# Half products for four of the `down` tiles and a third pair of `wno`, with two moved steps, in a one-core decoder layer

## The chip, the cores and the metric

The kernel runs on one core of one Trainium2 chip. The metric is the device time of one execution in microseconds (us). Three runs of the kernel before took 679.52, 680.35 and 680.2 us, so the median is 680.2 us.

The core has five engines with a queue each: TensorE (PE in the profile, its weight loads PEld), VectorE (DVE), ScalarE (ACT), GpSimd (POOL) and SyncE (SP). An engine works through its own queue in order, and waits at an instruction until the semaphores that this instruction names are there. Transfers are issued by SP and by POOL. TensorE writes its results into PSUM, eight banks per partition that hold 512 float32 values each; DVE and ACT read and write PSUM as well as SBUF.

## The reference

One decoder layer for 512 tokens of 1024 features: a norm, one wide projection, a pooling mixer and a sparse attention, gates that merge the two, an output projection, and a gated MLP with a short convolution. What the change touches:

```
x = x + (gate_pool * y_pool + gate_nsa * y_nsa) @ w_out      # y_nsa = heads @ w_nsa_out
h = rms_norm(x, ffn_norm_g)
gate_pre, val = split(h @ w_up)                              # 2 x 2816 columns
y = silu(causal_dwconv(gate_pre, conv_w, conv_b)) * val
x = x + y @ w_down                                           # 2816 = 22 tiles of 128 rows
```

All values are float32. The kernel keeps tokens in the free dimension, so a matrix is `out[128 features, 512 tokens] += w[128 x 128] x[128, 512]` over tiles of 128 features.

## The kernel before, in words

**Precision.** Every factor is split into a rounded high part and a low remainder (`split`: ACT makes the high part, DVE subtracts). A full-width step is then three matmuls of 512 columns: high by high, high by low, low by high (`mm3`). In some places the low part is made by a transfer that adds (`split_by_dma`: two ACT operations and a POOL transfer, nothing on DVE).

**Half products.** Some products are done two by two in Winograd's form of Strassen's scheme: a pair of output tiles, the contraction cut in two and the tokens cut in two, so that seven products of half the width (256 columns) stand where eight would. It needs sums of weight tiles and sums of input halves, which DVE makes. `product` runs one such half product: over `n` tiles, three matmuls of 256 columns each. A product whose `k0` is false does not begin a new sum, but adds to what lies in the bank; so ACT first copies an earlier product from its bank to the one that continues it. The MLP's `up` tiles 1 to 21 (`up_fast`), the last 8 of the 22 `down` tiles (`dz_fast`) and the first two of four pairs of `wno`, the attention's output projection (`FASTM = (0, 1)`), run so.

**The order of the `wno` and `out` stage.** The four pairs of `wno` come one after the other; a fast pair leaves its last two half products in `held`, to run inside the next pair. Each gives two merged tiles `mh[f]`, `ml[f]`, eight in all. `out` contracts over these eight. Its output tiles 0 and 4 begin with their weights and six of the eight steps each, then the last two steps follow (`begin`). After it come the norm's sum of squares, `norm_rstd` and `up` tile 0, which runs as two full products (`up_plain`): gate half, value half. Within the value half, after seven of its eight steps, TensorE broadcasts the norm's factor (`bcast_rstd`: `diag` tiles made by ACT and DVE, two matmuls, one ACT copy to `rb`).

**The order of the MLP.** `up` tiles 1 to 21 follow. `down` over its first 14 tiles is cut into `GROUPS`, of 5, 5 and 4 tiles; each group gives eight steps (`dn_group`), one per output tile: load the weights, split them, 15 (or 12) matmuls of 512 columns into the two-bank PSUM tile with the tag `sc`, and a DVE addition to `x2[f]`. A group is put on the list `fills` at the `up` tile given in `AT`, and `FILL` says how many steps of the list go before an `up` tile and at three places inside it, where TensorE has to wait for a copy otherwise. What is left of the list runs after `up` tile 21, and then `dz_fast` does the last 8 tiles. `y_sums` makes the sums of `y` halves that `dz_fast` needs.

**The planner.** No engine's order is written out fully. Every operation is noted with a price and with what it depends on (`Plan.note`), and `Plan.run` orders each engine's queue by due times; TensorE's order within the main stream is that of the program. PSUM tiles count as a whole in these dependences, unless their name is in `fine`; then it goes by columns. SBUF tiles come from 60 `page` buffers and three rings of three for weights (`wraw`, `whi`, `wlo`). `AHEAD` is the number of pages that must be left free when weights for half products are fetched ahead. All instructions are emitted at one place, so they all bear line 431 in the profile, and have to be told apart by their tiles.

Of the kernel before, what the change touches and what calls it, by code (L numbers as in the profile page):

```python
# [9 lines left out]
F32R = mybir.dt.float32r  # L10
I32 = mybir.dt.int32
AF = mybir.ActivationFunctionType
# [3 lines left out]
P = 128  # L16
T = 512
NT = 4
D = 1024
KD = 8  # L20
# [3 lines left out]
FF = 2816  # L24
KF = 22
LAST = 14
GROUPS = ((0, 5), (5, 10), (10, 14))
EPS = 1e-6
BIG = 1e30

# [23 lines left out]
RINGS = {"wraw": 3, "whi": 3, "wlo": 3}  # L54
PLAIN = (0,)
DIRECT = (0,)
FASTM = (0, 1)
AT = (6, 12, 16)
FILL = {f: (0, 0, 0, 0) for f in range(22)}
FILL.update({f: (0, 1, 1, 0) for f in (7, 10, 13, 16,)})  # L60
FILL.update({f: (0, 1, 0, 0) for f in (6, 8, 9, 11, 12, 14, 15, 17, 18, 19,)})
TRIES = 12
RESERVE = 3
CUTS = (1, 2)
# [4 lines left out]
SHARE = 1.5  # L69
LANDS = (0.8, 0.8, 1.2, 1.2, 2.0, 2.0)  # L70
TRIALS = ((0.5, RATE), (0.8, RATE), (1.4, RATE), (0.8, 0.9 * RATE))
AHEAD = 4
RUN = 12


# [357 lines left out]

@with_exitstack
def hybrid_layer(ctx: ExitStack, tc: tile.TileContext, xT, xa, pos, par, cst, poolw, w1, wa, wb, wf,
                 wpo, wno, wout, wup, wdn, wdz, out):
    nc = tc.nc
    pl = Plan(nc)
    PE, ACT, DVE, POOL, SP = pl.engines
# [8 lines left out]
    def page(name, shape=(P, T), dt=F32):  # L448
        return pl.tile(sb, shape, dt, name, "pg", PAGES)
# [59 lines left out]
    H2 = T // 2  # L509
# [18 lines left out]
    w2 = R("w2").rearrange("p (a b) -> p a b", a=2)  # L528
# [4 lines left out]
    pt = bank("mm")  # L533
# [61 lines left out]
    rb = keep("rb", (P, T))  # L595
# [42 lines left out]
    A, KQ, KH, KL = (ang[:, i] for i in range(4))  # L638
# [55 lines left out]
    for t in range(NT):  # L694
        pt = bank("mm")
# [593 lines left out]
    for f in (0, 4):  # L1289
        wh, wl = weights(flat(wout[f]), 1024, "v")  # L1290
        begin[f] = wh, wl, any_bank()
        mm3(begin[f][2], wh, wl, mh, ml, 0, 6, nk=KD)
    for f in (0, 4, 1, 5, 2, 6, 3, 7):
        xres = page("xres")
        with pl.behind(tail):
# [37 lines left out]
        ACT.activation(t, t, AF.Silu)  # L1333
        return t

    yth, ytl, ylast = {}, {}, {}

    def y_sums(k):
        b1, b2 = ylast[k], ylast[k + 4]
        ta, tb = page("ta"), page("tb")  # L1340
        DVE.tensor_sub(ta[:, :H2], b1[:, :H2], b1[:, H2:])
        DVE.tensor_sub(tb[:, :H2], b2[:, H2:], b1[:, H2:])
        DVE.scalar_tensor_tensor(ta[:, H2:], ta[:, :H2], -1.0, b2[:, H2:], op0=ALU.mult, op1=ALU.subtract)
        DVE.scalar_tensor_tensor(tb[:, H2:], ta[:, H2:], -1.0, b2[:, :H2], op0=ALU.mult, op1=ALU.subtract)
# [12 lines left out]
    def up_plain(f):
        pts = []
        for s in range(2):
            wh, wl = weights(flat(wup[f, s]), 1024, "v" if f in DIRECT else "d")  # L1360
            pt = any_bank()
            if f == 0 and s == 1:
                mm3(pt, wh, wl, gh, gl, 0, 7, nk=KD)
                bcast_rstd(rstd2, rb, "tr")
            mm3(pt, wh, wl, gh, gl, 7 if f == 0 and s == 1 else 0, KD)
            pts.append(pt)
            if s == 0:
                begun.append(pl.last())
            if f == 0 and s == 0:
                norm_rstd(acc, rstd2, bank("sc", (P, 2, T))[:, 0])  # L1370
        pg, pv = pts
        y, g = page("y"), page("fg")
        DVE.tensor_mul(g, pg, rb)
        t = conv(f, g, g)
        DVE.tensor_mul(y, pv, rb)
        DVE.tensor_mul(y, y, t)
        split_y(f, y)
# [20 lines left out]
    def dn_group(g):  # L1398
        lo, hi = GROUPS[g]

        def one(f, free):
            wh, wl = weights(wdn[f, :, lo * P:hi * P], (hi - lo) * P, "v")
            pt = any_bank() if free else bank("sc", (P, 2, T))[:, 0]
            mm3(pt, wh, wl, yh, yl, lo, hi, koff=lo, nk=hi, first=lo)
            DVE.tensor_add(x2[f], pt, x2[f])

        for f in range(KD):
            fills.append(lambda free, f=f: one(f, free))

    def half_weights(first, second, w, dma, gate):  # L1410
        rg, r1, r2 = ring("wraw"), soon("r1"), soon("r2")
# [74 lines left out]

    for f in range(KF):
        if f in AT:
            dn_group(AT.index(f))
        fill(FILL[f][0], True)  # L1490
        if f in PLAIN:
            up_plain(f)
        else:
            up_fast(f, *FILL[f][1:])
# [42 lines left out]
    pl.emit(TRIES, RESERVE)  # L1537


_INS = ["xT", "xa", "pos", "par", "cst", "poolw", "w1", "wa", "wb", "wf", "wpo", "wno", "wout", "wup", "wdn", "wdz"]  # L1540


def _layout(x, positions, mix_norm_g, w_in, q_norm_g, k_norm_g, cmp_pe, cmp_w1, cmp_w2, pool_w,
            pool_scale, w_pool_out, w_nsa_out, w_out, ffn_norm_g, w_up, conv_w, conv_b, w_down):
    import numpy as np

    f = lambda a: np.asarray(a)
    x, w_in = f(x)[0], f(w_in)[0]
    A = {}
    A["xT"] = x.T.reshape(KD, P, T)  # L1550
    p = f(positions)[0]
    cpos = np.zeros(P, p.dtype)
    idx = np.minimum(16 * np.arange(32) + 31, T - 1)
    cpos[:32] = p[idx]
    cpos[32:64] = p[idx]
    A["pos"] = np.concatenate([p.reshape(NT, P).T, cpos[:, None]], axis=1)

    def cols(a, n):
        return f(a)[0].reshape(n, P).T

    def stack2(a):
        return a.reshape(16, 2, DH, -1).transpose(1, 2, 0, 3).reshape(P, 16, -1)

    pe = np.stack([stack2(f(cmp_pe)[0, i][..., None])[..., 0] for i in range(2)], axis=1)
# [25 lines left out]
    A["cst"] = np.concatenate([cst[n_].astype(np.float32) for n_ in CST], axis=1)  # L1590
    A["poolw"] = f(pool_w)[0].transpose(1, 0, 2)
    kv = w_in[:, 1024:1792].reshape(D, 6, 128)
    wi = w_in.reshape(KD, P, -1)
    kvk = kv.reshape(KD, P, 6, 128)
    A["wa"] = np.concatenate([wi[:, :, 512:1024], kvk[:, :, 2], kvk[:, :, 4]], axis=2)
    wb = np.concatenate([kvk[:, :, 3], kvk[:, :, 5], wi[:, :, 1792:1816]], axis=2)
    A["wb"] = wb.transpose(1, 0, 2)

    def tiles(w):
        k, m = w.shape  # L1600
        return w.reshape(k // P, P, m // P, P).transpose(2, 1, 0, 3)

    A["wf"] = np.concatenate([tiles(kv[:, 0]), tiles(kv[:, 1]), tiles(w_in[:, :512]),
                              tiles(w_in[:, 1816:])])
    A["wpo"] = tiles(f(w_pool_out)[0]).reshape(4, 2, P, 4, P).transpose(0, 2, 1, 3, 4)
    A["wno"] = tiles(f(w_nsa_out)[0]).reshape(4, 2, P, 2, 2, P).transpose(0, 2, 1, 4, 3, 5).reshape(4, P, 8, P)
    A["wout"] = tiles(f(w_out)[0])
    A["wup"] = tiles(f(w_up)[0]).reshape(2, KF, P, KD, P).transpose(1, 0, 2, 3, 4)
    wd = tiles(f(w_down)[0])
    A["wdn"] = wd[:, :, :LAST].reshape(KD, P, LAST * P)  # L1610
    A["wdz"] = wd[:, :, LAST:]
    return {n_: np.ascontiguousarray(A[n_]) for n_ in _INS}

# [18 lines left out]
```

## Time and profile before

| | |
|---|---|
| median of three runs | 680.2 us (679.52 to 680.35) |
| the profiled execution's own time | 680.19 us |
| its span | 678.1 us |
| TensorE busy | 673.4 us, 4294 matmuls |
| DVE, ACT, POOL busy | 545.2, 458.7, 109.0 us |
| granted TensorE clock | 1.0 |

A row of the timeline gives start and length in us, engine, operation, output tile `<-` input tiles, sizes and the count; in brackets the idle time before it and what ended it. A row of the chain of waits gives start, length, and what ran. A row of the busy times by stretch gives the stretch, then per engine the busy time and the number of instructions. The tags `mm`, `tr`, `av` and `sc` are PSUM tiles. Busy times of TensorE's matmuls overlap, so the pace of matmuls is read from the chain, where a piece ends as the next begins.

### The profile page before, as it was taken

To read this page: it belongs to the slowest core of one execution; us is meant where nothing else is said; L and a number is where in the kernel's file an instruction comes from. 1 tells how busy PE (TensorE), PEld (TensorE's weight loads), DVE (VectorE), ACT (ScalarE), POOL (GpSimd) and SP (SyncE) were. 2 spreads that over 40 slices of the span, in tenths; PEclk is the share of its full clock that TensorE was granted. 3 is DMA by queue.
4 is the path that set the end of the run, shared out by engine and by line. 5 is a ranking of instruction groups with operands and counts; after the bars stand their busy time and mean duration, and the time that the engine had idled before them with its cause. 6 is when DMAs were issued, how large, how long until landed. Compare 5 with 4: busy or idle time off the path is not lost.

```text
span 678.1 us, 11960 instructions
## 1 busy us (share of the span) xinstructions
PE 673.4 (99%) x4294; PEld 609.1 (90%) x4294; DVE 545.2 (80%) x1198; ACT 458.7 (68%) x857; POOL 109.0 (16%) x138
## 2 busy tenths in 40 slices
PE   9999999999999999999999999999999999999998
PEld 8898888888888888988889999999999999999997
DVE  6869678788887867788888998887778787899983
ACT  7666577776677765347788867677657677675741
POOL 0010111010110110001322312222213122220121
PEclk9999999999999999999999999999999999999999
DMA  8469646263565555846977958779858678553774
GB/s 306 145 156 264 172 108 187 67 171 99 143 167 134 143 134 181 312 146 203 232 166 176 194 144 203 194 170 208 190 160 190 168 161 211 134 115 129 191 181 109
DMA packets 51179, 116.41 MB, mean 172 GB/s; under 512 B 5808, under 2 KB 9264, under 8 KB 51120
## 3 DMA queue, kind: packets, MB, share of 16 engines
q1 hardware_dynamic: 32688, 76.44, 33.9%
q0 software_dynamic: 18288, 39.07, 32.6%
q8 instruction: 34, 0.56, 0.3%
q14 instruction: 25, 0.20, 0.1%
q10 hardware_dynamic: 144, 0.14, 0.1%
HBM read 70.28 MB, written 6.29 MB: 113 GB/s over the span
## 4 chain that ended last, share of the span: by engine, by line
PE 99%; DMA 1%; SPq 0%; ACT 0%; DVE 0%; issue 0%
PE mm L431 38%; PE tr L431 36%; PE sc L431 13%; PE av L431 12%; DMA wraw<-wa 1%; SPq L431 0%; ACT whi L431 0%; DVE o L431 0%
## 5 line engine op out<-in xcount | busy, mean ns | idle before, releaser
L431 ACT ACTIVATE whi<-wraw 128x1024 fp32r<-128x1024 f32 (+4 forms) x99 | 91.9, 930 | 40.9 <-PE sc L431 14.7
L431 DVE TENSOR_TENSOR wlo<-wraw,whi 128x1024 fp32r<-128x1024 f32 (+3 forms) x73 | 74.0, 1015 | 5.1 <-ACT whi L431 4.3
L431 PE MATMUL tr<-tl,sh 128*128 128x256 f32 x261 | 73.1, 280 | 0.0
L431 PE MATMUL mm<-xh,whi 128*128 128x512 f32 x176 | 70.7, 402 | 0.0
L431 PE MATMUL tr<-th,sh 128*128 128x256 f32 x250 | 70.4, 282 | 0.0
L431 PE MATMUL tr<-th,sl 128*128 128x256 f32 x250 | 70.4, 282 | 0.0
L431 PE MATMUL mm<-xh,wlo 128*128 128x512 f32 x176 | 68.9, 391 | 0.0
L431 PE MATMUL mm<-xl,whi 128*128 128x512 f32 x176 | 68.6, 390 | 0.0
L431 POOL DMA_DIRECT2D sl<-r x46 | 39.8, 866 | 149.8 <-ACT sl L431 104.8
L431 POOL DMA_DIRECT2D wlo<-wraw x26 | 22.3, 858 | 231.7 <-ACT wlo L431 178.8
L431 PEld LDWEIGHTS tr<-tl,sh 128*128 128x128 f32 x261 | 49.3, 189 | 0.2
L431 PEld LDWEIGHTS tr<-th,sh 128*128 128x128 f32 x250 | 47.0, 188 | 0.7
L431 PEld LDWEIGHTS tr<-th,sl 128*128 128x128 f32 x250 | 47.0, 188 | 0.0
L431 ACT ACTIVATE wlo<-wraw 128x1024 fp32r<-128x1024 f32 x26 | 27.6, 1060 | 19.3 <-PE mm L431 18.4
L431 PEld LDWEIGHTS mm<-xh,wlo 128*128 128x128 f32 x176 | 33.0, 188 | 7.3
L431 PEld LDWEIGHTS mm<-xl,whi 128*128 128x128 f32 x176 | 33.1, 188 | 6.2
L431 ACT ACTIVATE pp<-pp,asm 128x384 f32<-128x384 f32 (+3 forms) x64 | 35.4, 556 | 4.9 <-DVE asm L431 4.9
L431 PEld LDWEIGHTS mm<-xh,whi 128*128 128x128 f32 x176 | 33.1, 188 | 6.1
L431 DVE SCALAR_TENSOR_TENSOR ft<-fg,pr,ft 128x511 f32<-128x511 f32 (+1 forms) x44 | 32.9, 749 | 7.0 <-ACT ft L431 6.3
L431 POOL DMA_DIRECT2D sl<-wraw x26 | 22.4, 862 | 84.7 <-ACT sl L431 68.5
L431 ACT ACTIVATE sh<-wraw 128x512 fp32r<-128x512 f32 x52 | 32.3, 620 | 4.1 <-DVE wraw L431 4.0
L431 ACT ACTIVATE sl<-r 128x512 fp32r<-128x512 f32 x46 | 28.6, 622 | 9.3 <-DMA r<-wup 5.4
(443 smaller groups left out, 2134.4 us busy)
## 6 DMA issues: line engine op xcount, KB each, us to landing
wlo<-wraw POOLq DMA_DIRECT2D x26, 512.0 KB, 4.6
wraw<-wup SPq DMA_DIRECT2D x23, 512.0 KB, 4.1
sl<-r POOLq DMA_DIRECT2D x46, 256.0 KB, 4.8
wraw<-wf SPq DMA_DIRECT2D x22, 512.0 KB, 3.6
r<-wup SPq DMA_DIRECT2D x42, 256.0 KB, 5.7
sl<-wraw POOLq DMA_DIRECT2D x26, 256.0 KB, 4.2
wraw<-wdn SPq DMA_DIRECT2D x16, 320.0 KB, 3.7
sl<-s POOLq DMA_DIRECT2D x17, 256.0 KB, 5.0
```

The lines of the kernel that those rows point to most:

```text
L431: getattr(self.real[o.eng], method)(*a, **kw)
```

## The change

1. `GROUPS` becomes 0 to 4, 5 to 8, 9 to 13. The middle group (four tiles) no longer runs through `dn_group` but through the new `hp_group`: for each of four pairs of output tiles seven half products of two tiles each, cut in four steps. All of a pair's products go to one two-bank tile `t` with the tag `sc`: `bx` and `bq` are the two halves of its first bank, `by` is the first half of its second bank. `t` is put in `fine`. `y_sums` also makes the sums of `y` halves for tiles 5 to 8. The weights come from a new input `wdh` that holds the same numbers as that part of `wdn`.
2. `FASTM` becomes (0, 1, 2): a third pair of `wno` runs by half products, the fourth stays full.
3. `out` tiles 0 and 4 begin with four steps of tile 0, four of tile 4, two of tile 0, two of tile 4, in place of six and six.
4. `bcast_rstd` comes after the value half of `up` tile 0 instead of before its last step.
5. `AT`, `FILL` and `AHEAD` are set anew. Steps of the list by `up` tile: before 6:1, 7:2, 8:1, 9:1, 10:2, 11:1, 12:1, 13:2, 14:1, 15:1, 16:2, 17:1, 18:1, 19:1, six left for the end; after 6:1, 7:2, 8:1, 9:2, 10:2, 11 to 14: three each, 15: four (the sixteen steps of the four pairs), 16 to 18: one each, five left for the end.

```diff
-GROUPS = ((0, 5), (5, 10), (10, 14))
+GROUPS = ((0, 5), (5, 9), (9, 14))
+HALVED = 1
-FASTM = (0, 1)
-AT = (6, 12, 16)
+FASTM = (0, 1, 2)
+AT = (6, 11, 16)
-AHEAD = 4
+AHEAD = 2
...
-        mm3(begin[f][2], wh, wl, mh, ml, 0, 6, nk=KD)
+    for k0, k1 in ((0, 4), (4, 6)):
+        for wh, wl, pt in begin.values():
+            mm3(pt, wh, wl, mh, ml, k0, k1, nk=KD)
...
-            if f == 0 and s == 1:
-                mm3(pt, wh, wl, gh, gl, 0, 7, nk=KD)
-                bcast_rstd(rstd2, rb, "tr")
-            mm3(pt, wh, wl, gh, gl, 7 if f == 0 and s == 1 else 0, KD)
+            mm3(pt, wh, wl, gh, gl, 0, KD)
             pts.append(pt)
...
+            if f == 0 and s == 1:
+                bcast_rstd(rstd2, rb, "tr")
...
+    def hp_group(g):
...
+            def one():
+                rg, hi, lw = ring("wraw"), ring("whi", F32R), ring("wlo", F32R)
+                SP.dma_start(rg, flat(wdh[c]))
+                split(hi[:, :T], lw[:, :T], rg[:, :T])
+                a11, a12, a21, a22 = (rg[:, q * H2:(q + 1) * H2] for q in range(4))
+                s3, e3, hi2, lo2 = soon("s3")[:, :H2], soon("sh", F32R), soon("sh", F32R), soon("sl", F32R)
+                DVE.tensor_add(s3, a11, a21)
+                DVE.tensor_add(a21, a21, a22)
+                DVE.tensor_add(a11, a11, a21)
+                DVE.tensor_add(a12, a12, a11)
+                split_by_dma(hi2, lo2, rg[:, T:])
+                split(hi[:, T:], lw[:, T:], rg[:, :T])
+                split(e3[:, Le], e3[:, Ri], s3)
...
+                t = bank("sc", (P, 2, T))
+                pl.fine.add(t.tensor.name)
+                bx, bq, by = t[:, 0, :H2], t[:, 0, H2:], t[:, 1, :H2]
+                b.extend((bx, bq, by))
+                product(bx, w[0], mv(0, 0), True, 2)
+                ACT.activation(by, bx, AF.Copy)
+                product(bq, w[2], mv(2, 0), False, 2)
+                DVE.tensor_sub(x2[e][:, Ri], x2[e][:, Ri], bq)
+
+            def two():
+                bx, bq, by = b
+                product(by, w[3], mv(2, 1), False, 2)
+                DVE.tensor_add(x2[f][:, Ri], x2[f][:, Ri], by)
+                product(bx, w[1], mv(1, 0), False, 2)
+                DVE.tensor_add(x2[f][:, Le], x2[f][:, Le], bx)
+
+            def three():
+                bx, bq, by = b
+                product(by, w[4], mv(3, 0), False, 2)
+                DVE.tensor_sub(x2[e][:, Ri], x2[e][:, Ri], by)
+                product(bq, w[5], mv(1, 1), False, 2)
+                DVE.tensor_add(x2[f][:, Ri], x2[f][:, Ri], bq)
+
+            def four():
+                product(b[2], w[6], mv(3, 1), False, 2)
+                DVE.tensor_sub(x2[e][:, Le], x2[e][:, Le], b[2])
```

More of the change, by code (lines that the diff above doesn't have):

```diff
@@ L56 @@
 DIRECT = (0,)
-FASTM = (0, 1)
-AT = (6, 12, 16)
+FASTM = (0, 1, 2)
+AT = (6, 11, 16)
 FILL = {f: (0, 0, 0, 0) for f in range(22)}
-FILL.update({f: (0, 1, 1, 0) for f in (7, 10, 13, 16,)})
-FILL.update({f: (0, 1, 0, 0) for f in (6, 8, 9, 11, 12, 14, 15, 17, 18, 19,)})
+FILL.update({f: (0, 1, 1, 0) for f in (7, 9, 10)})
+FILL.update({f: (0, 1, 0, 0) for f in (6, 8, 16, 17, 18)})
+FILL.update({f: (0, 1, 1, 1) for f in (11, 12, 13, 14)})
+FILL.update({15: (1, 1, 1, 1)})
 TRIES = 12
@@ L435, in hybrid_layer @@
 def hybrid_layer(ctx: ExitStack, tc: tile.TileContext, xT, xa, pos, par, cst, poolw, w1, wa, wb, wf,
-                 wpo, wno, wout, wup, wdn, wdz, out):
+                 wpo, wno, wout, wup, wdn, wdh, wdz, out):
     nc = tc.nc
@@ L1334, in conv, with y_sums @@
         return t
-    yth, ytl, ylast = {}, {}, {}
-    def y_sums(k):
-        b1, b2 = ylast[k], ylast[k + 4]
+    yth, ytl, ylast, ysh, ysl = {}, {}, {}, {}, {}
+    def y_sums(k, e, hi, lo, k0):
+        b1, b2 = ylast[k], ylast[e]
         ta, tb = page("ta"), page("tb")
@@ L1345, in y_sums @@
         for i, x in ((0, ta), (1, tb)):
-            yth[k - LAST, i], ytl[k - LAST, i] = page("yth", dt=F32R), page("ytl", dt=F32R)
-            split(yth[k - LAST, i], ytl[k - LAST, i], x)
+            hi[k - k0, i], lo[k - k0, i] = page("yth", dt=F32R), page("ytl", dt=F32R)
+            split(hi[k - k0, i], lo[k - k0, i], x)
     def split_y(f, y):
@@ L1351, in split_y @@
         split(yh[f], yl[f], y)
-        if f >= LAST:
+        h0, h1 = GROUPS[HALVED]
+        if f >= LAST or h0 <= f < h1:
             ylast[f] = y
+        if h0 + 1 < f < h1:
+            y_sums(f - 2, f, ysh, ysl, h0)
         if f > LAST + 3:
-            y_sums(f - 4)
+            y_sums(f - 4, f, yth, ytl, LAST)
     def up_plain(f):
@@ L1408, in dn_group, with mv, pair @@
             fills.append(lambda free, f=f: one(f, free))
+    def hp_group(g):
+        lo = GROUPS[g][0]
+        Le, Ri = slice(0, H2), slice(H2, T)
+        def mv(i, half):
+            c = slice(half * H2, (half + 1) * H2)
+            if i < 2:
+                return tuple((lambda k, q=q: q[lo + 2 * i + k][:, c]) for q in (yh, yl))
+            return tuple((lambda k, q=q: q[k, i - 2][:, c]) for q in (ysh, ysl))
+        def pair(c):
+            f, e, w = 2 * c, 2 * c + 1, []
+            b = []
+            def one():
[11 more added lines that the diff above has]
+                split(e3[:, Le], e3[:, Ri], s3)
+                w11, w12, w2, w4 = ((hi[:, q * H2:(q + 1) * H2], lw[:, q * H2:(q + 1) * H2]) for q in range(4))
+                w.extend((w11, w12, (hi2[:, Le], lo2[:, Le]), w2, (e3[:, Le], e3[:, Ri]), w4, (hi2[:, Ri], lo2[:, Ri])))
+                t = bank("sc", (P, 2, T))
[21 more added lines that the diff above has]
+                DVE.tensor_sub(x2[e][:, Le], x2[e][:, Le], b[2])
+            fills.extend((lambda free, q=q: q()) for q in (one, two, three, four))
+        for c in range(4):
+            pair(c)
@@ L1488, in hybrid_layer @@
         if f in AT:
-            dn_group(AT.index(f))
+            g = AT.index(f)
+            (hp_group if g == HALVED else dn_group)(g)
         fill(FILL[f][0], True)
@@ L1537, in hybrid_layer @@
     pl.emit(TRIES, RESERVE)
-_INS = ["xT", "xa", "pos", "par", "cst", "poolw", "w1", "wa", "wb", "wf", "wpo", "wno", "wout", "wup", "wdn", "wdz"]
+_INS = ["xT", "xa", "pos", "par", "cst", "poolw", "w1", "wa", "wb", "wf", "wpo", "wno", "wout", "wup", "wdn", "wdh", "wdz"]
 def _layout(x, positions, mix_norm_g, w_in, q_norm_g, k_norm_g, cmp_pe, cmp_w1, cmp_w2, pool_w,
@@ L1610, in _layout @@
     A["wdn"] = wd[:, :, :LAST].reshape(KD, P, LAST * P)
+    h0, h1 = GROUPS[HALVED]
+    A["wdh"] = wd[:, :, h0:h1].reshape(4, 2, P, h1 - h0, P).transpose(0, 2, 1, 3, 4).reshape(4, P, 2 * (h1 - h0), P)
     A["wdz"] = wd[:, :, LAST:]
```

## The prediction

> **What bounds the kernel now.** I read the page first, then what TensorE itself waited for, then the chain of waits in order of time, then the busy times by stretch, and last the timeline at the places that the change touches.
>
> ```profile
> span 678.1 us, 11960 instructions
> ...
> PE 673.4 (99%) x4294; PEld 609.1 (90%) x4294; DVE 545.2 (80%) x1198; ACT 458.7 (68%) x857; POOL 109.0 (16%) x138
> ...
> PE 99%; DMA 1%; SPq 0%; ACT 0%; DVE 0%; issue 0%
> ```
>
> The chain that ends last is TensorE from end to end. A busy matmul row doesn't prove it, since the rows overlap, so the next view asks what TensorE waited for (us in total, times, longest):
>
> ```profile
> PE mm L431 <- POOL ones L431: 1.0, 1, 1.0
> PE sc L431 <- ACT whi L431: 0.3, 1, 0.3
> ```
>
> These two are the whole answer, and both lie in the first 7 us. Everything after is paced by TensorE's own work: what the change saves there comes off the end one for one, and so does every new wait put on. The other engines cost nothing until they make TensorE late.
>
> The pace comes from the chain (start, length, what, count), where one piece ends as the next begins:
>
> ```profile
> 285.22 2.73 PE tr L431 x12
> ...
> 485.08 1.42 PE tr L431 x12
> 486.49 3.43 PE sc L431 x15
> ```
>
> A matmul of 512 columns takes 3.43 / 15 = 0.2287 us in a `down` step and 2.73 / 12 = 0.2275 in `wno`; one of 256 columns takes 1.42 / 12 = 0.1183 us.
>
> **TensorE's own work.** `down`: 8 outputs by 4 tiles by 3 passes, 96 matmuls of 512 columns, go: 96 x 0.2287 = 21.96 us. In come 4 pairs by 7 products by 2 tiles by 3 passes, 168 of 256 columns: 168 x 0.1183 = 19.87 us. That is -2.08 us. `wno`: 2 outputs by 4 tiles by 3 passes go, 24 x 0.2275 = 5.46 us; 7 by 2 by 3 come, 42 x 0.1183 = 4.97 us; -0.49 us. Regrouping the ten other `down` tiles, the new order in `out` and the moved broadcast leave the counts alone. Together -2.57 us.
>
> **A wait inside step one of each pair.** In `one`, the product into `bx` is followed on TensorE at once by the product into `bq`, and ACT copies `bx` to `by` meanwhile. `bx` and `bq` are different columns of one bank, so by columns nothing orders the copy and the second product. The trace has one place where two engines touch different columns of one bank: `mm`, from which ACT takes 256 columns into `vv`, ACT takes 24 others into `gates`, and DVE reads the 256 again.
>
> ```profile
> 43.92 0.47 ACT L431 ACTIVATE vv<-mm,rstd 128x256 fp32r<-128x256 f32 x1 [0.95 <-PE mm L431]
> 44.29 0.27 ACT L431 ACTIVATE gates<-mm,rhalf 128x24 f32<-128x24 f32 x1
> 44.59 0.48 DVE L431 SCALAR_TENSOR_TENSOR vv<-mm,rstd,vv 128x256 fp32r<-128x256 f32 x1 [0.93 <-ACT gates L431]
> ```
>
> DVE needs nothing of `gates`. Its input `vv` was there at 44.39, yet it starts at 44.59, just after `gates` ends at 44.56, and that is its named releaser. So accesses of two engines to one bank are ordered here even where the columns differ. That was two readers; I carry it over to a reader and TensorE's write, which no row of before shows. Then the `bq` product waits until the copy is done. The price, from rows where ACT makes the same copy (256 columns, bank to bank) after a product, and where TensorE resumes after ACT:
>
> ```profile
> 5.98 0.42 ACT L431 ACTIVATE whi<-wraw 128x256 fp32r<-128x256 f32 x1 [1.18 <-DMA wraw<-wa]
> 6.45 0.74 PE L431 MATMUL sc<-whi,xh 128*128 128x256 f32 x4 [0.35 <-ACT whi L431]
> ...
> 350.29 1.05 ACT L431 ACTIVATE whi<-wraw 128x1024 fp32r<-128x1024 f32 x1
> 350.51 0.68 DVE L431 TENSOR_TENSOR y<-tr,rb 128x512 f32<-128x512 f32 x1
> 351.06 0.28 PE L431 MATMUL mm<-gp,wlo 128*128 128x256 f32 x1
> 351.17 0.28 PE L431 MATMUL av<-th,sh 128*128 128x256 f32 x1
> 351.43 0.37 ACT L431 ACTIVATE tr<-mm 128x256 f32<-128x256 f32 x1
> ```
>
> The product's last matmul starts at 351.06, TensorE goes on at 351.17, and the copy runs from 351.43 to 351.80. TensorE resumes 0.05 us after ACT's end (6.40 to 6.45). So it would go on at 351.85 instead of 351.17: 0.68 us. Behind the waiting instruction stands all of TensorE's queue, and nothing else is there to run. Four pairs: +2.72 us. Bounds: nothing at all, if only readers are kept apart (a gain is excluded, as a wait gives no time); and, if a 1.05 us split begins on ACT just as the product ends, 1.05 more each, 6.9 us. I take 2.7, because the measured copy started promptly and the planner, which believes the copy due only for step two, leaves ACT free for a third of this stretch (below).
>
> By the Trainium skill (PSUM — Partial Sum Buffer, section "PSUM bank collisions raise a hardware error") two engines must be kept apart by bank and quadrant of partitions, not by address, reads included, TensorE's writes too. The trace agrees for the two readers (44.56 to 44.59); by this rule the sum holds the four waits, without it the `down` part would keep its full 2.08 us.
>
> The other accesses to `t` have room: between two steps of a pair run at least 12 matmuls, 1.42 us, and DVE drains such a bank sooner than that. Taken at 0.
>
> **DVE and ACT in the `down` stretch.** The stretch 470 to 540 holds what will be about `up` tiles 11 to 15 (columns: TensorE, its loads, DVE, ACT, POOL, clock, DMA share, GB/s):
>
> ```profile
> 262.00:281.50 19.50, 19.50 (x121) 17.45 (x120) 13.74 (x25) 8.51 (x15) 0.00 (x0) 1.00 0.71 246
> 281.50:300.70 19.20, 19.20 (x93) 16.17 (x92) 18.25 (x29) 7.77 (x11) 0.00 (x0) 1.00 0.54 194
> 350.00:390.00 40.00, 40.00 (x341) 40.00 (x340) 36.56 (x62) 33.46 (x62) 10.34 (x12) 1.00 0.82 182
> 400.00:470.00 70.00, 70.00 (x499) 65.83 (x498) 59.95 (x103) 49.98 (x89) 17.96 (x21) 1.00 0.76 178
> 470.00:540.00 70.00, 70.00 (x511) 66.35 (x510) 53.61 (x91) 46.51 (x83) 15.52 (x18) 1.00 0.78 186
> ```
>
> ```profile
> L431 DVE TENSOR_TENSOR x<-sc,x 128x512 f32<-128x512 f32 x18 | 12.4, 690 | 14.3 <-PE sc L431 14.2
> L431 DVE TENSOR_TENSOR wlo<-wraw,whi 128x640 fp32r<-128x640 f32 x16 | 13.1, 819 | 0.2 <-ACT whi L431 0.2
> L431 DVE TENSOR_TENSOR wlo<-wraw,whi 128x512 fp32r<-128x512 f32 x12 | 8.2, 684 | 0.1
> L431 DVE TENSOR_TENSOR fg<-mm,rb 128x256 f32<-128x256 f32 x21 | 8.8, 419 | 1.5 <-PE mm L431 1.5
> ```
>
> Out go six full steps of 0.69 + 0.82 = 1.51 us, 9.1 us. In come four pairs, each two 512-wide subtractions (1.37) and eleven 256-wide operations (four weight sums, the split of `s3`, six updates of `x2`; 11 x 0.42 = 4.62), 5.99 us, so 24.0. DVE goes from 53.6 to 68.5 us. TensorE needs 5 x 7 x 1.42 = 49.7 plus 19.9, 69.6 us, and 72.3 with the four waits. DVE would stand at 95%. It stood at 95% from 281.5 to 300.7 and at 91% from 350 to 390 with no gap on TensorE, and its work for `y` can run late. So 0, tightly; without that cover see the last rival. The sums for tiles 5 to 8 add 2 x (4 x 0.42 + 2 x 0.68) = 6.1 us to the stretch 400 to 470 (59.95 busy, and one more full step's 3.43 us of TensorE there): 0. ACT, even at DVE's durations, gets 4 x (5 x 0.69 + 2 x 0.42) = 17.2 us on its 46.5, 63.7 of 72.3, less what the full steps took: 0. The transfers carry the same bytes; POOL issues four more, on a queue busy 15.5 of 70 us. `up` tile 19 loses its full step, but TensorE met no wait before in tiles 20 and 21, which had none: 0. `AHEAD` and the new lists may reorder other queues anywhere; no gain is there to be had, since TensorE waits nowhere, and a loss I can't price: 0.
>
> **`wno` and `out`.** The third pair gives DVE 3 x 0.68 + 5 x 0.42 - 1.22 = 2.9 us more on weights (1.22: the 1024-wide subtraction below) and 6 x 0.42 - 2 x 0.69 = 1.1 more on results. The timeline's rows, two for this and two for the broadcast, and the two pieces of the chain that come after them:
>
> ```profile
> 298.81 1.22 DVE L431 TENSOR_TENSOR wlo<-wraw,whi 128x1024 fp32r<-128x1024 f32 x1
> 299.95 0.68 DVE L431 TENSOR_TENSOR ml<-tn,mh 128x512 fp32r<-128x512 f32 x1
> ...
> 347.38 1.13 DVE L431 SCALAR_TENSOR_TENSOR diag<-cs,rstd,diag 128x128 fp32r<-128x128 f32 x4
> 348.62 0.61 PE L431 MATMUL tr<-diag,ones 128*128 128x512 f32 x2
> ```
>
> ```profile
> 302.27 1.36 PE av L431 x6
> ...
> 352.75 1.41 PE tr L431 x12
> ```
>
> The last merged tile is ready at 300.63 and needed at 302.27: 1.6 us of slack, 1.1 once TensorE comes 0.5 earlier. The weight work fits into the 5.8 us that DVE has free from 262 to 281.5, the 1.1 us takes up the slack, and the weight split at 298.81 can come later. The new four-step order gives tiles 4 and 5, which now come last from the held products, 24 x 0.2275 = 5.46 us. Taken at 0; if the weight work falls into the dense stretch, 2.9 + 1.1 - 1.1 - 1.2 = 1.7 us.
>
> **The broadcast.** `diag` is done at 348.51, TensorE uses it at 348.62; 0.68 us later it has more room, but `rb` comes as much later, and DVE empties the two `tr` banks at 351.9 instead of 351.2, before TensorE comes back to them at 352.75. 0, between 0 and +0.7; a gain is excluded, as TensorE didn't wait there.
>
> **Sum**, against the profiled execution's own 680.19 us (span 678.1 and 2.1 around it; the median of 680.2 is the same): 680.19 - 2.08 - 0.49 + 2.72 = 680.3 us.
>
> **The rivals.** *The bank doesn't matter for TensorE's writes.* Then all 2.57 us come off: 677.6 us. For it: only readers are shown to be kept apart, and the planner's `fine` treats the halves as independent. Against it: the ordering at 44.59 had no need either.
>
> *DVE falls behind in tiles 11 to 15*, and the bank waits stay. The place is the steps two to four of a pair, whose products wait until DVE has read the bank. If DVE keeps up no more than the 91% of 350 to 390, its 68.5 us take 75.3 where TensorE has 72.3: +3.0, 683.3 us. It decides from the point at which DVE's tolerable share is under 95%. For it: the planner holds these reads due late, since it knows only columns. Against it: 281.5 to 300.7, and weight work can be done ahead or `y` work after.
>
> **How the numbers follow.** About 0.2%, 1.36 us, is what a measurement of this kernel can tell from no change: 678.84 to 681.56. The bank wait has 0.55; alone it gives 679.8 (copies prompt, resumption quicker) to 681.4 (an ACT operation ahead in one or two). The bank-free case has 0.25, all faster. DVE or late merged tiles on top have 0.20, mostly slower. A little of the first case spills to either side: faster 0.26, same 0.53, slower 0.21. The likeliest is 680.3; the range has to reach both rivals, 677.4 to 682.6, leaving out the worst of the third.
>
> **What would show it.** Matmuls: 4294 - 120 + 210 = 4384. TensorE's waits: four new ones on ACT for the `sc` tile, near 0.7 us each, between the first and second group of six matmuls of a pair; none elsewhere, in particular none on DVE in tiles 11 to 15 and none for `mh` in `out`. The prediction is wrong if the second six follow the first at 0.118 us, or if waits on DVE add up to more than 1 us.

## The result, and the profile after

The changed kernel takes 684.43 us (median of six runs, 682.73 to 686.34), the kernel before 680.08 us beside it (six runs). The ratio is 1.0064, 95% interval 1.0047 to 1.0081: slower by 0.6%, where I had forecast no change. The profiled execution took 684.47 us.

The page, and the whole answer to what TensorE waited for (us in total, times, longest):

```profile
span 682.7 us, 12240 instructions
...
PE 673.4 (99%) x4384; PEld 612.4 (90%) x4384; DVE 562.5 (82%) x1257; ACT 468.5 (69%) x883; POOL 112.5 (16%) x142
```

```profile
PE sc L434 <- DVE x L434: 2.0, 3, 1.0
PE sc L434 <- ACT sc L434: 1.4, 3, 0.5
PE tr L434 <- ACT u L434: 1.2, 2, 0.7
PE mm L434 <- POOL ones L434: 1.0, 1, 1.0
```

4384 matmuls are there, as counted. The busy time of TensorE, 673.4 us as before, tells nothing here, because its rows overlap. What is new are the first three lines of the waits. I counted the ACT waits, but neither the DVE waits nor those for `u`. This view counts a wait from the modelled end of the last matmul; measured from start to start of neighbouring matmuls, less their usual 0.118 us, and with the slow restart behind it (last section), each is about 0.27 us longer. Nine such gaps lie behind the first 7 us, 7.2 us in all. The kernel before has none there. With the 2.57 us that I had counted off TensorE's work, the span would be 678.1 - 2.57 + 7.2 = 682.7 us, and that is what was measured: the gaps account for the whole loss.

They are of three kinds.

**The four step ones.** The chain of waits in the first pair, `one` from its start to its last matmul (start, length, what):

```profile
477.05 0.72 PE sc L434 x6
477.77 0.02 issue
477.79 0.38 ACT sc L434
478.17 0.04 issue
478.21 0.98 PE sc L434 x6
```

Six matmuls of the product into `bx`, then ACT's copy to `by`, then six of the product into `bq`, which the copy has nothing to do with. This is the wait I forecast. It stands in three of the four pairs (behind 477.5, 496.3 and 514.8) and costs 0.72 to 0.73 us each time. In the fourth pair ACT makes the copy behind both products, and nothing waits.

**Step two, in two of the four pairs.** The timeline of the third pair's:

```profile
520.78 0.28 PE L434 MATMUL sc<-yth,wlo 128*128 128x256 f32 x1
...
520.90 0.28 PE L434 MATMUL sc<-yh,whi 128*128 128x256 f32 x1
...
521.14 0.28 PE L434 MATMUL sc<-yh,wlo 128*128 128x256 f32 x1
521.46 0.42 DVE L434 TENSOR_TENSOR x<-x,sc 128x256 f32<-128x256 f32 x1 [0.89 <-PE sc L434]
...
521.93 0.39 PE L434 MATMUL sc<-yh,whi 128*128 128x256 f32 x1 [0.51 <-DVE x L434]
```

Count the matmuls. The first six (to 520.78) are the product into `by`. The next three, from 520.90, are the first half of the product into `bx`, and its other three start at 521.93. In between DVE reads `by`, in the other bank. Its input is complete at 521.06 (520.78 + 0.28), yet it starts at 521.46, when the three `bx` matmuls have ended (521.42). And the next three wait for it. So DVE waits for a product that it doesn't read, and TensorE waits for a read of a bank that it doesn't write. Both accesses are to one tile, `t`. This costs 0.78 us, here and at 538.2.

**Four waits elsewhere.** In these ACT or DVE comes late to something that TensorE needs: 0.81, 0.41 and 0.96 us for ACT inside `up` tiles (behind 387.2, 398.0 and 590.0) and 1.29 us for DVE at the start of pair 4 (behind 531.5). The last and the third of these, from the timeline:

```profile
531.99 0.42 DVE L434 TENSOR_TENSOR fg<-tr,rb 128x256 f32<-128x256 f32 x1 [1.86 <-DMA sl<-r]
532.33 0.41 DVE L434 TENSOR_TENSOR x<-x,sc 128x256 f32<-128x256 f32 x1
532.79 0.39 PE L434 MATMUL sc<-yh,whi 128*128 128x256 f32 x1 [1.02 <-DVE x L434]
```

```profile
587.80 0.63 ACT L434 ACTIVATE yh<-y 128x512 fp32r<-128x512 f32 x1 [2.49 <-DMA sl<-r]
...
590.51 0.36 ACT L434 ACTIVATE u<-tr 128x256 f32<-128x256 f32 x1
...
590.92 0.39 PE L434 MATMUL tr<-th,sh 128*128 128x256 f32 x1 [0.69 <-ACT u L434]
```

Read the brackets from the bottom up. TensorE waits for DVE's `x`, which stands in DVE's queue behind `fg`; and `fg` waits 1.86 us for a transfer `sl<-r`. It uses nothing that this transfer brings, so only its own output can tie it to it: `fg` is to be written to a page in which `r` still lies, from which the transfer reads. In the second fence ACT's `yh` waits in the same way, and what is queued behind it, `u` among it, is late.

The other two look different. ACT's rows before the `u` of 388.0 and before that of 398.3:

```profile
381.82 0.64 ACT L434 ACTIVATE sl<-r 128x512 fp32r<-128x512 f32 x1 [2.80 <-DMA r<-wup]
...
387.60 0.36 ACT L434 ACTIVATE u<-tr 128x256 f32<-128x256 f32 x1
```

```profile
396.44 1.06 ACT L434 ACTIVATE whi<-wraw 128x1024 fp32r<-128x1024 f32 x1 [1.61 <-DMA wraw<-wup]
...
397.93 0.36 ACT L434 ACTIVATE u<-av 128x256 f32<-128x256 f32 x1
```

Here ACT waited for the weights that it was to split, and not for a page to come free; from there to `u` its queue ran without a pause. In the first of the two ACT worked for 5.8 us in between, so whether that wait or the order of the queue made `u` late isn't shown.

**What went as forecast elsewhere.** The chain at the start of the norm, before and after:

```profile
343.07 0.79 PE sc L431 x8
```

```profile
342.34 0.79 PE sc L434 x8
```

The norm begins 0.7 us earlier, and no wait stands between `wno` and the broadcast. Of this 0.08 us was there at 259 us already (the same piece of 60 matmuls begins at 259.24 against 259.32), and neither kernel has a gap between there and the norm. So the third pair brought 0.65 us, 0.16 more than the 0.49 that I had counted.

### The profile page after: what moved, and what is told of

It is laid out like the page before. It is cut to its first block, busy times and chain, and to the rows that moved or that the text cites. A ratio compares the mean times of both kernels' runs of the same rounds, so it can differ in the third digit from the quotient of the medians.

```text
span 682.7 us, 12240 instructions
## 1 busy us (share of the span) xinstructions
PE 673.4 (99%) x4384; PEld 612.4 (90%) x4384; DVE 562.5 (82%) x1257; ACT 468.5 (69%) x883; POOL 112.5 (16%) x142
## 4 chain that ended last, share of the span: by engine, by line
PE 91%; DMA 4%; ACT 2%; DVE 1%; issue 1%; POOL 0%; SPq 0%; POOLq 0%; ACTq 0%; DVEq 0%
PE mm L434 37%; PE tr L434 30%; PE av L434 13%; PE sc L434 12%; DMA r<-wup 2%; DMA sl<-r 2%; ACT sh L434 0%; ACT ft L434 0%; DVE ft L434 0%; POOL sl L434 0%; ACT sl L434 0%; ACT whi L434 0%; SPq L434 0%; DVE x L434 0%; ACT sc L434 0%
## 5 line engine op out<-in xcount | busy, mean ns | idle before, releaser
L434 POOL DMA_DIRECT2D sl<-wraw x30 | 25.9, 864 | 98.2 <-ACT sl L434 79.8
L434 ACT ACTIVATE sh<-wraw 128x512 fp32r<-128x512 f32 x57 | 35.4, 621 | 4.3 <-DVE wraw L434 3.9
L434 PE MATMUL tr<-gh,whi 128*128 128x256 f32 (+1 forms) x184 | 35.7, 291 | 0.0
L434 PE MATMUL av<-tl,sh 128*128 128x256 f32 x121 | 34.0, 281 | 0.0
L434 ACT ACTIVATE sh<-r 128x512 fp32r<-128x512 f32 x50 | 31.0, 619 | 1.9 <-issue 1.0
L434 PE MATMUL av<-th,sh 128*128 128x256 f32 x110 | 31.1, 283 | 0.1
L434 PE MATMUL av<-th,sl 128*128 128x256 f32 x110 | 31.0, 282 | 0.0
L434 PE MATMUL tr<-tl,sh 128*128 128x256 f32 x110 | 30.9, 281 | 0.0
```

The lines of the kernel that those rows point to most:

```text
L434: getattr(self.real[o.eng], method)(*a, **kw)
```

## The experiments

All runs stand beside runs of the kernel before (680.04 to 680.15 us). "Gaps" are TensorE's gaps behind the first 7 us of the profiled execution, counted as above.

| run | us (range, runs) | ratio to before (95%) | gaps, us |
|---|---|---|---|
| the change | 684.43 (682.73-686.34, 6) | 1.0064 (1.0047-1.0081) | 7.2 |
| e1_reads_behind | 679.42 (678.52-681.9, 12) | 0.9991 (0.9983-0.9999) | 2.7 |
| e2_down_only | 685.64 (684.3-689.0, 6) | 1.0088 (1.0070-1.0106) | 7.9 |
| e3_wno_only | 680.48 (680.08-681.11, 11) | 1.0006 (0.9997-1.0015) | 1.2 |
| e4_before_ahead2 | 680.5 (679.71-680.93, 11) | 1.0003 (0.9994-1.0011) | 0.5 |
| e5_by_own_tile | 681.22 (680.25-681.93, 10) | 1.0017 (1.0008-1.0027) | 4.0 |
| e6_bq_own_tile | 682.06 (678.44-685.23, 10) | 1.0031 (1.0012-1.0050) | 4.9 |
| e7_before_58_buffers | 680.91 (679.58-681.82, 10) | 1.0009 (1.0000-1.0018) | 0.8 |
| e8_behind_s3_apart | 682.38 (680.68-683.22, 5) | 1.0032 (1.0019-1.0044) | 4.4 |
| e9_behind_u_apart | 678.6 (677.84-680.09, 11) | 0.9980 (0.9972-0.9989) | 2.0 |
| e10_u_apart | 683.08 (681.79-686.57, 6) | 1.0056 (1.0037-1.0075) | 4.9 |
| e11_behind_u_ahead3 | 682.08 (680.42-684.84, 10) | 1.0032 (1.0022-1.0041) | 4.3 |
| e12_tries10 | 677.91 (676.98-678.71, 10) | 0.9970 (0.9961-0.9980) | 1.4 |
| e13_tries8 | 678.3 (677.56-679.77, 8) | 0.9975 (0.9965-0.9985) | 1.2 |
| e14_tries14 | 677.95 (676.75-679.41, 5) | 0.9972 (0.9957-0.9986) | 1.8 |
| e15_behind_tries8 | 678.36 (677.96-678.91, 10) | 0.9977 (0.9968-0.9986) | 1.0 |
| e16_behind_tries10 | 679.44 (678.8-682.33, 10) | 0.9998 (0.9987-1.0009) | 2.1 |
| e17_before_u_apart | 679.91 (679.17-680.18, 10) | 0.9998 (0.9988-1.0007) | 0 |

My theory from the trace of the change: the accesses to `t` are ordered as a whole and in the order in which they are emitted, so a read that the planner puts between two halves of a product stops TensorE; and the rest is ACT and DVE held up behind transfers. The rival: DVE is simply too heavily loaded in this stretch.

### The reads moved behind the second product (e1_reads_behind)

`pl.behind(pl.last())` lets an operation be emitted only behind the one named.

```diff
                 product(bx, w[0], mv(0, 0), True, 2)
-                ACT.activation(by, bx, AF.Copy)
                 product(bq, w[2], mv(2, 0), False, 2)
+                with pl.behind(pl.last()):
+                    ACT.activation(by, bx, AF.Copy)
...
                 product(by, w[3], mv(2, 1), False, 2)
-                DVE.tensor_add(x2[f][:, Ri], x2[f][:, Ri], by)
                 product(bx, w[1], mv(1, 0), False, 2)
+                with pl.behind(pl.last()):
+                    DVE.tensor_add(x2[f][:, Ri], x2[f][:, Ri], by)
```

and likewise for the first read of step three.

> The changed kernel with one difference: in a pair's steps one, two and three, the copy or the read that stood between two products now comes behind the second of them. In the trace of the changed kernel TensorE waits nine times after its first 7 us, 6.3 us in all and about 0.1 us more at each restart: five of them (3.2 us) stand in the middle of a pair's two products, for ACT or DVE; one (1.2) stands before the first product of the last pair, for a DVE queue that itself waited for a transfer out of a buffer; three (1.9) are for ACT's copies in the up tiles. Theory 1, the order in which the instructions stand on the PSUM tile: the five waits vanish, 3.2 + 0.5 = 3.7 us, and the time falls from 684.4 to about 680.7. Theory 2, DVE and ACT are too busy there (rival): the waits move to the next product and the time stays within 1 us of 684.4.

679.42 us: five less than the change, with the same operations. The five waits inside the steps of the pairs made 3.7 us of that; the rest lies outside them, in an order that is another one everywhere. No gap stands inside a step of a pair any more. The profiled execution was the slowest of the twelve (681.9 us); it has two gaps, 0.58 us behind 382 and 2.09 us at 485. The second, in the timeline:

```profile
485.12 0.43 DVE L434 TENSOR_TENSOR s<-wraw 128x256 f32<-128x256 f32 x1 [2.94 <-DMA sl<-s]
485.46 0.42 DVE L434 TENSOR_TENSOR x<-x,sc 128x256 f32<-128x256 f32 x1
```

DVE stands idle for 2.94 us until a transfer has read the buffer that it wants to write `s` to, and the read of `sc` is queued behind. So it is not the DVE load that stops TensorE here.

### One part of the change at a time (e2_down_only, e3_wno_only, e4_before_ahead2)

e2 is the change without the third pair and without the new beginning of `out`; e3 is the kernel before with only these two; e4 is the kernel before with only the smaller `AHEAD`.

```diff
# e2, against the change
-FASTM = (0, 1, 2)
+FASTM = (0, 1)
...
# e3, against before
-FASTM = (0, 1)
+FASTM = (0, 1, 2)
...
# e4, against before
-AHEAD = 4
+AHEAD = 2
```

> The changed kernel without the third wno pair and without the new beginning of out, so with the half products for down alone (the moved broadcast stays). If the third wno pair brings its arithmetic, 0.49 us, this one takes 684.9; if the late merged tiles cost what it saves, 684.4; the waits in the down stretch stay by every theory, at 5 to 7 us.

> The kernel before with the third wno pair and the new beginning of out alone. 24 matmuls of 512 columns become 42 of 256: 680.1 - 0.5 = 679.6 if nothing waits for the merged tiles; 680.1 or more if DVE delivers them late.

> The kernel before with AHEAD at 2 instead of 4 and nothing else: fetches ahead may take all but two of the 60 buffers. Theory 3, the buffers: ACT and DVE then have to write into buffers that a transfer is still reading, and wait for it to land, as the changed kernel's rows show three times (2.5, 1.9 and 0.2 us on ACT and DVE). If AHEAD alone does that, TensorE shows such waits here too, 1 to 3 us, and the time is 681 to 683; if it needs the sums for tiles 5 to 8 as well, which hold eight more buffers, the time stays at 680.1.

e2 takes 685.64 us: so the loss is there with the half products for `down` alone. It has three waits for ACT of 0.72 us, three for DVE in mid-product of 0.78, and three elsewhere in the MLP, up to 1.83. e3 gives 680.48: the norm begins at 341.94, so the third pair takes its half microsecond off, but a reordered MLP gives it back in two waits, 0.42 us behind 387 and 0.53 behind 607. The parts don't simply add: whatever changes the list of operations gives a new order everywhere. e4 is the same as before.

### One product in a PSUM tile of its own (e5_by_own_tile, e6_bq_own_tile)

`by`, or `bq`, goes to the one-bank tile `av`, and `up` tiles 11 to 16 rotate over the other five banks. In e6 the product into `bq` begins a new sum.

```diff
# e5 (the other tiles' turn left out)
...
-                bx, bq, by = t[:, 0, :H2], t[:, 0, H2:], t[:, 1, :H2]
+                bx, bq, by = t[:, 0, :H2], t[:, 0, H2:], bank("av")[:, :H2]
...
# e6 (likewise)
...
+                bx, bq, by = t[:, 0, :H2], bank("av")[:, :H2], t[:, 1, :H2]
...
-                product(bq, w[2], mv(2, 0), False, 2)
+                product(bq, w[2], mv(2, 0), True, 2)
```

> The changed kernel with one thing moved: `by` lies in the PSUM tile `av`, by itself, and the up tiles meanwhile take turns on the five others; bx and bq stay in one bank of `t`. Nothing is held behind anything. In the changed kernel DVE's read of by, in the second bank of t, and the product into bx, in its first bank, waited for each other twice (0.78 us each). If what orders them is the tile, these waits in step two go away and the waits on ACT's copy in step one (0.73 each, three or four) stay, since bx and bq still share t: 1.6 us less, about 682.9, if the buffers cost the same. If it were the bank alone, by was in a bank of its own before, so that the waits in step two would stay.

> The counterpart: `bq` lies in the tile `av` by itself, and bx and by stay in the two banks of `t`. Either theory (tile or bank) lets the product into bq run beside ACT's copy: the waits in step one go (three of 0.73 us, 2.2 in all, about 682.2). By the tile theory the waits in step two, for DVE's read of by between the two halves of the product into bx, stay or grow in number (0.78 each); by the bank theory there are none.

In e5 the four step ones wait, and no step two does (the waits, then the timeline in the first pair):

```profile
PE sc L434 <- ACT av L434: 1.8, 4, 0.5
```

```profile
476.32 0.37 ACT L434 ACTIVATE av<-sc 128x256 f32<-128x256 f32 x1 [0.49 <-PE sc L434]
...
476.74 0.39 PE L434 MATMUL sc<-yth,sh 128*128 128x256 f32 x1 [0.46 <-ACT av L434]
```

In e6 it is the other way round. ACT copies while TensorE runs the product into `bq`, and a step two still waits in the middle:

```profile
476.83 0.37 ACT L434 ACTIVATE sc<-sc 128x256 f32<-128x256 f32 x1 [0.18 <-PE sc L434]
...
476.87 0.28 PE L434 MATMUL av<-yth,sl 128*128 128x256 f32 x1
...
533.50 0.41 DVE L434 TENSOR_TENSOR x<-x,sc 128x256 f32<-128x256 f32 x1
...
533.96 0.39 PE L434 MATMUL sc<-yh,whi 128*128 128x256 f32 x1 [0.79 <-DVE x L434]
```

So with the two in different tiles neither wait is there: no step two of four waits in e5, no step one of four in e6. With the two in one tile step one waits four times out of four in e5, and step two once in e6, twice in the change and four times in e10 (below), as the order of that kernel puts the read in mid-product or behind it. That the tile of its own lets both run at once is seen in e5's first pair, where DVE reads `by` from `av` while the product into `bx` goes on:

```profile
481.46 0.28 PE L434 MATMUL sc<-yh,whi 128*128 128x256 f32 x1
...
481.54 0.41 DVE L434 TENSOR_TENSOR x<-x,av 128x256 f32<-128x256 f32 x1
481.58 0.28 PE L434 MATMUL sc<-yl,whi 128*128 128x256 f32 x1
```

In step two of the change `bx` and `by` lie in different banks of one tile, and that is not enough. The unit of the order is the tile, not the bank.

The Trainium skill (PSUM — Partial Sum Buffer, section "PSUM bank collisions raise a hardware error") asks for guards by bank and quadrant of partitions. By it step one has to wait and step two hasn't; the measured 0.78 us of step two shows that this program keeps accesses apart more widely than that.

Both medians lie below the change, e6's with a wide spread (678.44 to 685.23), and neither reaches e1: e6 has 1.76 and 2.10 us behind 585 and 607 for ACT's `u`. Five `up` banks in place of six may be part of it; this wasn't separated.

### Fewer buffers (e7_before_58_buffers), and pages given back (e8, e9, e10, e17)

e7 takes two of the 60 pages from the kernel before (with `AHEAD` at 2). The others take something out of the pages and put it where the norm's constants lie, which nothing reads by then: e8 the pair's `s3`, e9 the halves `u2` and `u3` of the `up` tiles. e10 is the latter on the change itself, e17 on the kernel before.

```diff
# e7, against before
-PAGES = 60
+PAGES = 58
-AHEAD = 4
+AHEAD = 2
...
# e8, against e1
-                s3, e3, hi2, lo2 = soon("s3")[:, :H2], soon("sh", F32R), soon("sh", F32R), soon("sl", F32R)
+                e3, hi2, lo2 = soon("sh", F32R), soon("sh", F32R), soon("sl", F32R)
+                s3 = pl.tile(sb, (P, T), F32, "s3", "t_cs", 1)[:, :H2]
...
# e9 against e1, e10 against the change, e17 against before
+    uts = []
...
-        half = [page("u1")]
-        u2, u3 = half[0][:, :H2], half[0][:, H2:]
+        if not uts:
+            uts.append(pl.tile(sb, (P, 3 * H2), F32, "u1", "t_cs", 1))
+        u2, u3 = uts[0][:, f % 2 * H2:(f % 2 + 1) * H2], uts[0][:, T:]
```

> The kernel before with AHEAD at 2 and 58 buffers instead of 60. With 60 and AHEAD at 2 it took 680.5, and TensorE waited 0.2 us. Theory 3, the buffers: two fewer put more of ACT's and DVE's work behind transfers that still read a buffer, so that rows of ACT and DVE that wait for a transfer into sl come up, and TensorE waits 0.5 to 3 us, 681 to 683.5. Theory 2, the load of DVE and ACT: nothing changes, as their work is the same, 680.5.

> The kernel of e1 (reads behind the second product; 679.4) in which the weight sum s3 of the four pairs takes the place of the constants, which are done with by then, instead of one of the 60 buffers. In the profile of e1 TensorE lost 2.1 us once, where DVE stood 2.9 us before it could write an s3, since a transfer still read that buffer. Theory 3: that wait can't come up there any more, and the time falls by 0.3 to 1.5 us, to 678 to 679.1. If the wait only moves to the next instruction that takes a buffer, it stays at 679.4.

> The kernel of e1 (reads behind the second product) in which ACT's copies u2 and u3 of every up tile lie in the place of the constants, which are done with by then, and not in one of the 60 buffers. In e8 and e6 TensorE's longest waits (2.1 and 1.8 us) were for such a copy, which stood behind a transfer that still read its buffer. Theory 3, the buffers: ACT's row u no longer waits for a transfer, TensorE's waits for ACT's u go, and a page per up tile is free for the rest: 677.7 to 679.0, with less spread than e8 (680.7 to 683.2). Theory 2, the load of ACT and DVE: the same work stays, so the waits for u stay, 679.4 to 682.4.

> The changed kernel with u2 and u3 in the place of the constants and nothing else; the reads in a pair stay where the change put them. Theories 1 and 3 together: the waits in the middle of a pair's products stay (three to five, 2.2 to 3.7 us), those for ACT's u go (2.2 us): 684.4 falls to 681 to 682.5. If the buffers don't matter, 684.4.

> The kernel before with u2 and u3 in the place of the constants. TensorE waits nowhere in it after the first 7 us, so a freed buffer has nothing to give: 680.0 +- 0.5. If it fell by 1 us or more, the gain of e9 would not come from the half products, but from u alone.

e7: from 345 to 610 us ACT and DVE wait longer for transfers that read their buffers (6.3 us in all, 1.0 before, 2.6 in e4), but TensorE loses only 0.8 us, and the time is 680.91. e17 is 679.91: giving pages to the kernel before brings nothing, as it has no wait to lose.

e9 is 678.6 us, and clearly faster than before (0.9972 to 0.9989). e10, with the pages but with the reads where the change has them, is 683.08:

```profile
PE sc L434 <- DVE x L434: 2.1, 4, 0.5
...
PE sc L434 <- ACT sc L434: 0.5, 1, 0.5
```

Four mid-product waits of 0.78 us and a step one of 0.73 are back. So the place of the reads is the larger cause: with it the same pages give 678.6 in place of 683.08.

e8 was a miss, 682.38 us, though it has more free pages than e1 (its profiled execution was the fastest of five, 680.68). The rows of its waits show the known picture, ACT behind a transfer and TensorE behind ACT (TensorE's waits, then ACT's from 345 to 610 us):

```profile
PE tr L434 <- ACT u L434: 2.3, 3, 1.8
```

```profile
ACT u L434 <- DMA sl<-r: 2.9, 1, 2.9
```

And e9 has long waits behind transfers too (ACT 3.6 us, DVE 5.1 in the same stretch) and loses little by them. So their total alone doesn't decide the time; in the rows above it is what stands in the queue behind them that makes TensorE late.

The busy times from 470 to 545 us bear on the rival of the load (columns: TensorE, its loads, DVE, ACT, POOL, clock, DMA share, GB/s): before, after, e9.

```profile
470.00:545.00 75.00, 75.00 (x545) 71.02 (x544) 58.18 (x99) 50.89 (x92) 17.20 (x20) 1.00 0.75 182
```

```profile
470.00:545.00 75.00, 71.58 (x583) 69.88 (x582) 62.97 (x124) 54.57 (x102) 19.86 (x23) 1.00 0.78 177
```

```profile
470.00:545.00 75.00, 74.66 (x627) 74.26 (x626) 66.03 (x131) 54.34 (x102) 19.73 (x23) 1.00 0.80 185
```

In the 75 us from 470 DVE is busy for 62.97 us in the slow kernel and for 66.03 us in the faster one, which gets more done (627 matmuls against 583). DVE was not the bound; in the slow kernel it was waiting.

### More weights held back (e11_behind_u_ahead3), and other orders (e12 to e16)

e11 is e9 with one more page kept free of early weights. `TRIES` is the number of orders the planner tries; another number gives another order of the same operations. e12, e13 and e14 are e9 with 10, 8 and 14 in place of 12; e15 and e16 are e1 with 8 and 10.

```diff
# e11, against e9
-AHEAD = 2
+AHEAD = 3
...
# e12 (e13: 8, e14: 14), against e9; e15 (8) and e16 (10), against e1
-TRIES = 12
+TRIES = 10
```

> The kernel of e9 with AHEAD at 3, for which the buffers now suffice. One more buffer is left free for the work of the moment, at the price of later fetches: by theory 3 fewer waits of ACT and DVE for transfers into sl than in e9, and a time at or under e9's; if fetches come too late, TensorE waits for weights instead and the time is 1 us higher.

> The kernel of e9 (678.6) with the planner's number of tries at 10 instead of 12: the same work, buffers and rules, in another order on DVE, ACT and SP. It measures what the order alone is worth. If the differences between e1, e8, e9 and e11 (679.4, 682.4, 678.6, 682.1) are due to what each changed in the buffers, this stays within 0.5 us of 678.6. If they are largely the chance of the order that the planner finds, whose reckoning doesn't hold the transfers' landing well, it lies anywhere from 678 to 682.5, and its TensorE waits, if any, stand again behind ACT or DVE instructions that wait for a transfer into sl.

> As e12 with 8 tries: a third order of the same kernel. Buffers as such: 678.6 +- 0.5. Chance of the order: 678 to 682.5, with waits behind transfers into sl.

> As e12 with 14 tries: a fourth order of the same kernel. Buffers as such: 678.6 +- 0.5. Chance of the order: 678 to 682.5, with waits behind transfers into sl.

> The kernel of e1 (u still in the 60 buffers) with 8 tries: another order of it. The four orders with u apart took 677.9 to 678.6. If the buffer of u is what makes TensorE wait, the orders of e1 lie above them, 679 to 683, with rows of ACT's u or DVE's first weight sums waiting for a transfer into sl; if e1's 679.4 was only a bad order, this takes 677.9 to 678.6.

> As e15 with 10 tries, a third order of the kernel of e1: 679 to 683 by the buffers, 677.9 to 678.6 by the chance of the order.

e11 was a miss: 682.08 us, where e9 has 678.6, with five gaps of up to 1.6 us (one behind a transfer of weights, two behind ACT operations that had waited 3.00 and 2.94 us for transfers). With `u` apart, e9's operations give 677.91, 678.3, 677.95 and 678.6 in four orders; with `u` in the pages, e1's give 678.36, 679.42 and 679.44 in three. So the order alone is worth about 1 us, and the place of `u` about 0.9 on the mean (678.19 against 679.07), less than the spread of e1's three.

e12 beats both kernels: 677.91 us, 0.3% below before (0.9961 to 0.9980) and 6.5 us below the change. 680.04 - 677.91 = 2.1 of the 2.57 us that I had counted for TensorE's work. Behind the first 7 us this view names only two of its waits:

```profile
PE av L434 <- ACT u L434: 0.4, 1, 0.4
PE mm L434 <- DVE y L434: 0.2, 1, 0.2
```

**What stays open.** Why e8 is 3 us slower than e1, and e11 3.5 us slower than e9. Both show gaps of the known kind, but whether the free pages or the order that the planner happened to find put them there, no run tells apart: every change of the pages changes the order too. For the same reason the 3.5 us of the four waits elsewhere in the changed kernel aren't split into `AHEAD`, the new lists and chance. By the rows above two of them come from ACT or DVE behind a transfer that held a page, one follows ACT's wait for weights, and for one the cause isn't shown.

## Why the prediction was wrong, point by point

- *TensorE's own work, -2.57 us*: right. The span of 682.7 us less the 7.2 us of gaps is 2.6 below the 678.1 of before, and e12 brings 2.1 to the end.
- *The wait in step one, 0.68 us each, +2.72*: the mechanism was right, and so nearly was the size: 0.72 to 0.73 each. It came in three pairs, 2.2 us, as one copy fell behind both products by itself. In e5 all four are there. But I put it down to the bank, and e6 with step two shows that it is the tile.
- *"The other accesses to `t` have room ... Taken at 0"*: this step failed. I looked at the distance from one step to the next, 12 matmuls, and not at the order within a step. DVE's read of the first product is emitted before the second has been finished, and within one tile TensorE stops for it: 1.6 us here, 3.1 in e10 with four. My own sign of being wrong, waits on DVE of more than 1 us, came with 2.0. I had the reason in hand: I had written that the planner's `fine` treats the halves as independent, and had used it only for the planner's due times. A planner that believes two things independent may put one anywhere, between the halves of the other too.
- *"`AHEAD` and the new lists may reorder other queues anywhere; ... a loss I can't price: 0"*: failed too, and was the larger sum: 1.29 + 0.81 + 0.41 + 0.96 = 3.5 us. I had excluded a gain, and a term that can only be a loss isn't rightly 0, priced or not. e3, e8 and e11 have gaps of 1.2 to 4.4 us, none of them for a read of `t`.
- *DVE and ACT in the stretch, 0*: right as to their load, though the working was off; the 1.29 us for DVE at the start of pair 4 comes from a transfer. I had DVE at 95%; it is at 84% (62.97 of 75) and at 88% in e9. Part of it is that rows of DVE overlap: the row of 1.22 us at 298.81, quoted in the prediction, is followed after 1.14 us by the next, and a sum of durations counts the rest twice.
- *The rival of the DVE load, 683.3 us*: its time was the nearest to the result, but not its mechanism. Waits of TensorE on DVE were there, 2.0 us, yet DVE was idle or had its input early in each of them, and a kernel with more DVE work is the fast one.
- *`wno`, `out` and the broadcast, 0 beyond the 0.49*: right as to waits; TensorE has no gap from 262 us to the norm, nor at the broadcast. The third pair itself brought 0.65.
- *The rival in which the bank doesn't matter, 677.6 us*: it didn't come. e12 with 677.91 comes near its time, because the reads there no longer stand between the products.

Sum: 680.3 forecast, + 1.6 (step two) + 3.5 (elsewhere) - 0.5 (one step-one wait fewer) = 684.9, against 684.43.

## What to carry to other kernels

In a program like this one, where two products share a PSUM tile, the order in which their reads and writes are emitted is an order in time, whatever the columns or banks: emit a read behind every product that must not wait for it, or give it a tile of its own. If a planner is told that parts of a tile are independent while the program still guards the whole, it may put a read between the halves of a product, and a count of instructions won't show it. When a change touches the list that a planner orders, try a few orders of the same operations before judging it: here they alone moved the time by about 1 us, and the gain of the change at its best (e12) is 2.1.

## What the runs showed of the hardware that was not expected

**A gap of 2.1 us can halve TensorE's clock behind it.** The busy times around the gap of e1 at 485 us, then those around a gap of 2.07 us in e16 at 484 (the column before the last two is the granted clock):

```profile
485.00:487.30 2.30, 0.48 (x5) 0.27 (x3) 2.18 (x6) 1.42 (x3) 0.08 (x1) 1.00 0.86 188
487.30:490.00 2.70, 2.70 (x18) 2.70 (x19) 2.29 (x7) 2.48 (x4) 0.86 (x1) 0.72 0.70 149
490.00:492.00 2.00, 2.00 (x11) 2.00 (x11) 1.26 (x3) 0.29 (x2) 0.00 (x0) 0.53 1.01 283
```

```profile
486.50:488.00 1.50, 1.50 (x13) 1.50 (x12) 1.17 (x3) 1.26 (x3) 0.86 (x1) 0.79 0.38 141
488.00:490.00 2.00, 2.00 (x12) 2.00 (x10) 1.86 (x5) 0.95 (x1) 0.00 (x0) 0.50 0.86 182
490.00:492.00 2.00, 2.00 (x15) 2.00 (x15) 1.08 (x3) 1.34 (x3) 0.00 (x0) 0.80 0.74 211
```

At half clock the lost shares make a slow stretch of 2 x (2.7 x 0.28 + 2.0 x 0.47) = 3.4 us in e1 and 2 x (1.5 x 0.21 + 2.0 x 0.50 + 2.0 x 0.20) = 3.4 us in e16. In it about sixteen matmuls of 256 columns start 0.213 us apart in place of 0.118, in both runs. That is 1.5 us lost on top of the gap: the 2.1 us wait costs 3.6. It doesn't happen each time: behind gaps of 2.08 us in e8 (at 605) and 2.10 us in e6 (at 607) the matmuls go on at 0.118 us. By the Trainium skill (TensorE: Matmul & The Clock Gate, section "What's actually happening") the clock falls after at least one idle window of about 3.4 us, and the window runs freely. The length of the slow stretch agrees with that window; the idle time doesn't, since 2.1 us sufficed twice.

**A wait costs more than the wait.** The timeline of the changed kernel, behind the first pair's step one:

```profile
478.21 0.39 PE L434 MATMUL sc<-yth,sh 128*128 128x256 f32 x1 [0.46 <-ACT sc L434]
...
478.44 0.28 PE L434 MATMUL sc<-ytl,sh 128*128 128x256 f32 x1
...
478.56 0.28 PE L434 MATMUL sc<-yth,sl 128*128 128x256 f32 x1
```

Behind the stop the second matmul starts 0.23 us after the first, the third 0.12 after the second. So each of the stops above cost about 0.11 us more than the delay of its first matmul.
